# Storing a convolution tail and final states untransposed, and a key weight laid out by numpy, in a hybrid SSD and MLA decode step

## The chip, the cores and the metric

One core of a Trainium2 chip runs the whole program. The metric is device time in microseconds (us) of one execution. Work done by numpy on the host, before the inputs are handed over or after the outputs come back, is not in it. The kernel before was run three times: 1915.88, 1918.3 and 1923.65 us, median 1918.3.

## The reference, cut to what matters

Two layers follow each other, each as `h = h + Mixer(RMSNorm(h))`: a Mamba-2 SSD layer and an MLA attention layer. Both run on a prompt of 1024 positions and on 8 samples of 8 positions. Three pieces of the reference matter here:

```
xbc, new_buf = causal_conv(xbc, conv_buf, conv_w, conv_b)    # new_buf: last 3 rows before the convolution, 4096 channels
y, new_state = ssd_scan(xs, dt, a_head, bm, cm, ssm_state)   # new_state: (heads 32, headdim 64, state 128)
q_lat = einsum('bqhn,chn->bqhc', q_nope, w_uk)               # absorb: the samples' queries into the latent space
```

`new_buf` and `new_state` are outputs, for the prompt (3 rows, one state) and for the samples (8 times 3 rows, 8 states). `w_uk` has the shape (256 latent, 16 heads, 64).

## The kernel before, in words

TensorE (PE) multiplies float32 by splitting each operand into a high and a low part and adding three products; these are the matmuls of `mm3` (L89) and `mm_tok` (L101). Transposes are matmuls against the identity `k.ident` in plain float32.

**SSD layer.** The 2048 channels and 32 heads fall into 8 groups. `Group` projects one group: four blocks of 128 channels (B, C, two of x) through `proj_piece` (tile `pj`, L89), each put into a `raw` tile, convolved on DVE (L528), and its last 3 rows of the prompt and of each sample copied by POOL into `ct`, 128 channels x 4 blocks x 27 rows (L521, L522). After the fourth block `conv_out` transposes the four pieces of `ct` to rows (tile `ctp`, L536), copies them to `co` on DVE (L538), and stores `co` by six DMAs of the SP queue (L541, L542). Then `gates` projects z (tile `pz`, L101). While group g+1 is projected, `ssd_chunks` and `ssd_states` scan group g: eight chunks of 128 positions, then the samples. The running state `S` (128 state rows x 4 heads x 64) is, after the eighth chunk, transposed in two pieces (tile `pf`, L669), copied to `fo` by ACT (L671) and stored (L672). `ctp`, `pf` and the scan's own transposes share PSUM slots with the tag `tr`, two of them in this layer; `co` takes one of the two slots of the tag `raw`. During the last group `last_steps` loads pieces of the output weight (tile `wor`, L772) into slots of the same tag `raw`, and ACT and DVE split them (L773, L774).

**MLA layer.** `Heads.prep_q` prepares one head at a time: it transposes the samples' queries (tile `qs`, L1357), transposes the head's 256 x 64 key weight out of the tile `wkr` in two pieces into the same PSUM tile (L1359), copies the result to `wt` on ACT (L1366), transposes the prompt's queries (L1374) and last multiplies `wt` by the samples' queries (tile `ql...p`, L1380). `wt` has two buffers, so head h takes the buffer of head h-2. `wkr` is loaded once per four heads (L1282) into a single buffer, and is also split into high and low parts for the prompt's keys. `maxpass` takes row maxima, turns them with a transpose (tile `nmp`, L1417) and sends them through DRAM on the SP queue: a store `nd<-nr` (L1421) and a load `qTh<-nd` (L1422) that waits for it.

**What sets the order.** In the SSD layer and in the first part of MLA a scheduler orders every engine's instructions when the program is built. In the head loop (`mla_heads`) and after it PE and POOL keep the order in which the code is written; ACT, DVE and the SP queue are still ordered by the scheduler. Nearly all DMAs are issued by SP, in order: an issue that waits for a semaphore holds up all that stand behind it.

Of the kernel before, what the change touches and what calls it, by code (L numbers as in the profile page):

```python
# [8 lines left out]
F32 = mybir.dt.float32  # L9
# [13 lines left out]
DIN = 2048  # L23
# [7 lines left out]
RAW = 3 + SEQ + NB * (NT + 3)  # L31
# [51 lines left out]
PB = dict(PB1)  # L83
# [44 lines left out]
def split(k, hi, lo, src, eng=None, parts=0):  # L128
    nc = k.nc
    k.cast = nc.scalar.copy(hi, src)  # L130
    n = parts and hi.shape[1] // parts
    for a in range(parts):
        s = slice(a * n, a * n + n)
        (eng or nc.vector).tensor_tensor(lo[:, s], src[:, s], hi[:, s].bitcast(F32), op=ALU.subtract)
    if not parts:
        return (eng or nc.vector).tensor_tensor(lo, src, hi.bitcast(F32), op=ALU.subtract)  # L136
# [324 lines left out]
class Group:  # L461
# [69 lines left out]

    def conv_out(self):
        k, g, nc, gp = self.k, self.g, self.k.nc, self.gp
        p = self.psum.tile([128, 512], F32, tag="tr", name=f"ctp{g}", bufs=PB["tr"])
        for bi in range(4):
            nc.tensor.transpose(p[:27, bi * 128 : bi * 128 + 128], self.ct[:, bi], k.ident)  # L536
        co = self.rp.tile([128, RAW], F32, tag="raw", name=f"co{g}", bufs=2)[:27, :512]
        nc.vector.tensor_copy(co, p[:27])  # L538
        sc = k.O["s_conv"].rearrange("o b w c -> (o b w) c")
        for o, n, c in ((0, 128, DIN + 128 * g), (128, 128, DIN + 1024 + 128 * g), (256, 256, 256 * g)):  # L540
            nc.sync.dma_start(k.O["p_conv"][0, 0, :, c : c + n], co[0:3, o : o + n])  # L541
            nc.sync.dma_start(sc[:, c : c + n], co[3:27, o : o + n])  # L542

    def steps(self):
        yield from self.pair(0, self.g == 0)
# [37 lines left out]
def ssd_chunks(k, gr, pools):  # L583
    nc, I = k.nc, k.I
    sp, psum = pools
    g = gr.g
    S = None
    hs = slice(4 * g, 4 * g + 4)
    for i in range(9):
# [5 lines left out]
        tag = f"{g}_{i}"  # L595
        p = psum.tile([128, 512], F32, tag="tr", name="trp" + tag, bufs=PB["tr"])
# [45 lines left out]
        if not smp:  # L642
# [12 lines left out]
            S = S2  # L655
# [8 lines left out]
        nc.scalar.activation(xD[:m], y[:m], AF.Square, accum_out=k.yssq[:m, i, g : g + 1])  # L664
        nc.sync.dma_start(k.y_d[sl, 256 * g : 256 * g + 256], y[:m])
        if i == 7:
            pf = psum.tile([128, 512], F32, tag="tr", name="pf" + tag, bufs=PB["tr"])
            for pr in range(2):
                nc.tensor.transpose(pf[:, pr * 128 : pr * 128 + 128], S[:, pr * 128 : pr * 128 + 128], k.ident)  # L669
            fo = sp.tile([128, 256], F32, tag="fo", name="fo" + tag, bufs=1).rearrange("p (a n) -> p a n", a=2)  # L670
            nc.scalar.copy(fo, pf[:, :256].rearrange("p (a n) -> p a n", a=2))  # L671
            nc.sync.dma_start(k.O["p_ssm"][0, 0, 4 * g : 4 * g + 4].rearrange("(a h) p n -> (h p) a n", h=2), fo)  # L672
        yield


# [64 lines left out]
def ssd_scan(k, gr, pools):  # L740
    chunks, states = ssd_chunks(k, gr, pools), ssd_states(k, gr, pools)
    for c in SCAN:
        next(chunks if c == "c" else states)
        yield 21 / len(SCAN)
    drain(chunks)
    drain(states)
# [437 lines left out]
class Heads:  # L1184
# [161 lines left out]
    def prep_q(self, h):  # L1346
        k, nc, sp = self.k, self.k.nc, self.sp
        hg, pr, j = h // 4, h // 2, h % 2
        if j == 0 and pr < 2:
            self.load_q(pr)  # L1350
        if j == 1 and 0 < pr < 7:
            self.load_q(pr + 1)
        qt = self.qts[pr]
        if h == 2:
            nc.gpsimd.memset(self.qT[2][1][96:98].bitcast(F32), 0.0)
        p = self.wt(f"qs{h}")
        nc.tensor.transpose(p[:96, :64], qt[:64, 8, 96 * j : 96 * j + 96], k.ident[:64, :64])  # L1357
        for c in range(2):
            nc.tensor.transpose(p[:64, 128 + c * 128 : 256 + c * 128],  # L1359
                                self.wkr[:, c, 64 * (h % 4) : 64 * (h % 4) + 64], k.ident)  # L1360
        qsn = sp.tile([64, 64], F32, tag="qsn", name=f"qsn{h}", bufs=2)
        nc.vector.tensor_copy(qsn, p[:64, :64])
        qv = k.qpr[:, :, NT * h : NT * h + NT]
        split(k, qv[0:32], qv[64:96], p[64:96, :64].rearrange("p (b t) -> p b t", t=NT))
        wt = sp.tile([64, 256], F32, tag="wt", name=f"wt{h}", bufs=2)
        nc.scalar.copy(wt, p[:64, 128:384])  # L1366
        yield
        if 1 < h < 4:
            self.ones_rows(h)
        qh, ql = self.q_of(h)  # L1370
        for c in range(2):
            p = self.wt(f"qT{h}{c}")
            for i in range(4):
                nc.tensor.transpose(p[:96, i * 128 : i * 128 + 128], qt[:, 4 * c + i, 96 * j : 96 * j + 96], k.ident)  # L1374
            cs = slice(512 * c, 512 * c + 512)
            split(k, qh[:96, cs], ql[:96, cs], p[:96])
            yield
        pl = self.wt(f"ql{h}p")
        for c in range(2):
            nc.tensor.matmul(pl[:, c * 64 : c * 64 + 64], wt[:, c * 128 : c * 128 + 128], qsn,  # L1380
                             start=True, stop=True)
        src = pl[:, :128].rearrange("p (c b t) -> p c b t", c=2, t=NT)
        split(k, *(x[:, :, :, NT * h : NT * h + NT] for x in (k.qlh, k.qll)), src)
        yield
# [684 lines left out]
def consts():  # L2069
# [21 lines left out]
_INS = ["x_prompt", "x_sample", "state_ssm", "state_conv", "cache_ckv", "cache_kpe", "page_table", "norm_w",  # L2091
        "final_norm_w", "ssd_w_in", "ssd_conv_w", "ssd_conv_b", "ssd_dt_bias", "ssd_a_log", "ssd_d", "ssd_norm_w",
        "ssd_w_out", "mla_w_in", "mla_q_norm_w", "mla_kv_norm_w", "mla_w_uq", "mla_w_uk", "mla_w_uv", "mla_w_out"]
_OUTS = [("y_prompt", (1, 1024, 1024)), ("y_sample", (8, 8, 1024)), ("p_ssm", (1, 1, 32, 64, 128)),
         ("p_conv", (1, 1, 3, 4096)), ("p_ckv", (1, 1, 1024, 256)), ("p_kpe", (1, 1, 1024, 32)),
         ("s_ssm", (1, 8, 32, 64, 128)), ("s_conv", (1, 8, 3, 4096)), ("s_ckv", (1, 8, 8, 256)),
         ("s_kpe", (1, 8, 8, 32))]


# [26 lines left out]
```

## Time and profile before

| | |
|---|---|
| three runs | 1915.88, 1918.3, 1923.65 us; median 1918.3 |
| profiled execution | span 1915.0 us from its first to its last instruction; the page prints no time around the span |
| PE busy | 1887.4 us, 99% of the span, 12023 matmuls |
| PE weight loads (PEld) busy | 1728.1 us, 90% |
| DVE, ACT, POOL busy | 1208.5, 1101.1, 823.3 us (63%, 57%, 43%) |
| granted TensorE clock, mean | 0.997 |

A matmul's record runs from its start to a modelled end, and the next matmul may start long before that end. So the busy time says that PE is nearly always holding some matmul, and what one matmul costs in a full stream is read from the distance of starts, not from the record's length. A line of the page such as L89 can be a helper's line, used by many tiles.

### The profile page before, as it was taken

What the parts mean: (1) busy time and instruction counts of PE and PEld (TensorE: products, weight loads), DVE (VectorE), ACT (ScalarE), POOL (GpSimd) and SP (SyncE); (2) the same over time, 40 slices, a digit from 0 to 9 for tenths busy, and PEclk for the clock granted to TensorE, in tenths of its full rate; (3) what the DMA queues carried; (4) which work ended last, traced back from release to release, by engine and by line L of the source; (5) the groups of instructions that cost most, each with busy time, mean ns of one, the idle gap of its engine ahead of it and who ended that gap; (6) DMA issues with size and microseconds to landing.
All of it is one profiled execution on the core that took longest, in us unless ns stands there. A gap on an engine that the chain in (4) does not pass through costs nothing.

```text
span 1915.0 us, 33672 instructions
## 1 busy us (share of the span) xinstructions
PE 1887.4 (99%) x12023; PEld 1728.1 (90%) x12023; DVE 1208.5 (63%) x2500; ACT 1101.1 (57%) x2528; POOL 823.3 (43%) x1116
## 2 busy tenths in 40 slices
PE   8999999999999999999999999999999999999998
PEld 7999999999999999888788998898888887888887
DVE  5557676757676767765534214566887878666665
ACT  6467666767666666732214323436777777755552
POOL 2447555555655555453004322103443434764551
PEclk9999999999999999999999999999999999999999
DMA  5223323332323232644424662233111112664451
GB/s 165 54 79 91 94 83 94 88 106 83 101 84 99 85 99 78 212 158 175 166 110 133 209 226 75 69 110 95 47 52 41 53 41 58 228 204 142 146 170 37
DMA packets 183967, 212.51 MB, mean 111 GB/s; under 512 B 19148, under 2 KB 147928, under 8 KB 182776
## 3 DMA queue, kind: packets, MB, share of 16 engines
q1 hardware_dynamic: 177304, 185.32, 31.1%
q0 software_dynamic: 6416, 24.91, 3.8%
q8 instruction: 95, 1.56, 0.3%
q14 instruction: 72, 0.59, 0.1%
q10 hardware_dynamic: 80, 0.13, 0.0%
HBM read 151.76 MB, written 58.52 MB: 110 GB/s over the span
## 4 chain that ended last, share of the span: by engine, by line
PE 90%; DMA 3%; DVE 3%; ACT 3%; issue 1%; POOL 0%; SPq 0%; POOLq 0%; DVEq 0%; ACTq 0%
PE pj L89 24%; PE pz L101 8%; PE pq L101 6%; PE pob L101 5%; PE p L101 5%; PE poa L101 4%; PE py L640 3%; PE sc L89 3%; PE o L89 2%; PE sc L1402 2%; PE o L1465 2%; PE o L1467 2%; PE st L1434 2%; PE st L1435 2%; PE st L1436 2%; PE o L1466 2%
## 5 line engine op out<-in xcount | busy, mean ns | idle before, releaser
L89 PE MATMUL pj<-xl,wih 128*128 128x384 f32 (+1 forms) x768 | 255.4, 333 | 0.0
L89 PE MATMUL pj<-xh,wih 128*128 128x384 f32 (+1 forms) x768 | 252.9, 333 | 1.2 <-ACT xh L276 0.8
L89 PE MATMUL pj<-xh,wil 128*128 128x384 f32 (+1 forms) x768 | 252.9, 329 | 0.0
L1448 POOL TENSOR_TENSOR tl<-P,th 128x384 fp32r<-128x384 f32 (+1 forms) x96 | 90.6, 944 | 232.3 <-ACT P L1446 186.6
L528 DVE SCALAR_TENSOR_TENSOR acc<-raw,vec,acc 128x1112 f32<-128x1112 f32 x96 | 141.6, 1476 | 15.3 <-ACT acc L524 14.4
L89 PEld LDWEIGHTS pj<-xh,wih 128*128 128x128 f32 x768 | 143.8, 188 | 2.6 <-ACT xh L276 1.4
L89 PEld LDWEIGHTS pj<-xl,wih 128*128 128x128 f32 x768 | 144.5, 188 | 1.0
L89 PEld LDWEIGHTS pj<-xh,wil 128*128 128x128 f32 x768 | 144.5, 188 | 0.5
L101 PE MATMUL pz<-wih,xh 128*128 128x256 f32 x504 | 143.3, 288 | 1.4 <-ACT z L569 1.4
L101 PE MATMUL pz<-wil,xh 128*128 128x256 f32 (+1 forms) x504 | 139.8, 283 | 0.0
L1445 ACT ACTIVATE th<-st 128x512 fp32r<-128x512 f32 x192 | 94.6, 493 | 66.6 <-PE st L1441 50.9
L101 PE MATMUL pz<-wih,xl 128*128 128x256 f32 x448 | 128.5, 287 | 0.0
L1733 POOL TENSOR_TENSOR kvl<-pgr,kvh 128x256 fp32r<-128x256 f32 x128 | 97.8, 791 | 70.6 <-ACT kvh L1731 70.3
L635 ACT ACTIVATE M<-M,tok 128x128 f32<-128x128 f32 (+1 forms) x288 | 90.4, 386 | 51.4 <-DVE M L631 51.2
L136 DVE TENSOR_TENSOR wil<-wraw,wih 128x512 fp32r<-128x512 f32 x88 | 74.4, 851 | 38.2 <-ACT wih L130 31.7
L101 PEld LDWEIGHTS pz<-wih,xh 128*128 128x128 f32 x504 | 95.9, 190 | 2.3 <-ACT z L569 1.8
L1446 ACT ACTIVATE P<-st 128x512 f32<-128x512 f32 x192 | 93.5, 487 | 0.0
L101 PEld LDWEIGHTS pz<-wil,xh 128*128 128x128 f32 (+1 forms) x504 | 92.8, 184 | 0.1
L101 PE MATMUL p<-w,oh 128*128 128x512 f32 (+3 forms) x304 | 88.8, 386 | 0.6 <-DVE h L1983 0.6
L616 POOL TENSOR_TENSOR xdd<-xsT,tok 128x256 f32<-128x256 f32 x64 | 50.0, 781 | 86.4 <-ACT xsT L602 83.3
L101 PEld LDWEIGHTS pz<-wih,xl 128*128 128x128 f32 x448 | 85.4, 191 | 0.7
L1448 DVE TENSOR_TENSOR tl<-P,th 128x512 fp32r<-128x512 f32 x96 | 72.1, 752 | 18.9 <-ACT P L1446 18.7
(830 smaller groups left out, 6212.5 us busy)
## 6 DMA issues: line engine op xcount, KB each, us to landing
wraw<-in_ssd_w_in SPq DMA_DIRECT2D x92, 256.0 KB
M<-acs_d SPq DMA_DIRECT2D x64, 256.0 KB
s<-in_state_ssm SPq DMA_DIRECT2D x32, 256.0 KB
y_d<-y SPq DMA_DIRECT2D x64, 128.0 KB
out_s_ssm<-s SPq DMA_DIRECT2D x32, 256.0 KB
q_d<-qt SPq DMA_DIRECT2D x32, 192.0 KB
qp<-q_d SPq DMA_DIRECT2D x8, 768.0 KB
wraw<-in_ssd_w_out SPq DMA_DIRECT2D x10, 512.0 KB
```

The lines of the kernel that those rows point to most:

```text
L89: nc.tensor.matmul(out, a, b, start=(i == 0), stop=(i == n - 1))
L101: nc.tensor.matmul(o, a, b, start=(j == 0), stop=(j == len(ops) - 1))
L136: return (eng or nc.vector).tensor_tensor(lo, src, hi.bitcast(F32), op=ALU.subtract)
L528: last = nc.vector.scalar_tensor_tensor(acc, raw[:, j : j + n], k.convw[j][:, blk : blk + 1], acc, op0=ALU.mult, op1=ALU.add)
L616: nc.gpsimd.tensor_tensor(v3(xdd), v3(xsT), hb(2), op=ALU.mult)
L635: nc.scalar.activation(M[:m, h, :m], M[:m, h, :m], AF.Exp, bias=tk[:, 0, 4 * g + h : 4 * g + h + 1])
L640: nc.tensor.matmul(py[:m, h * 64 : h * 64 + 64], M[:m, h, :m], xsT[:m, h * 64 : h * 64 + 64], start=True, stop=True)
L1402: nc.tensor.matmul(ps[:, :n], qh[:96, 128 * i : 128 * i + 128], kh[:96, 512 * c : 512 * c + n], start=True, stop=True)
L1445: nc.scalar.activation(th[:, :n], ps[:, :n], AF.Exp, scale=SCALE)
L1446: nc.scalar.activation(P[:, :n], ps[:, :n], AF.Exp, scale=SCALE)
L1448: eng.tensor_tensor(tl[:, :n], P[:, :n], th[:, :n].bitcast(F32), op=ALU.subtract)
L1733: nc.gpsimd.tensor_tensor(rl[:, j], raw[:, j], rh[:, j].bitcast(F32), op=ALU.subtract)
```

## The change

Three transposes leave the chip. `conv_out` now only stores `ct` as it lies, with one DMA per group, into a new output `conv` of shape (8, 128, 4, 27); numpy takes `p_conv` and `s_conv` out of it. The final state `S` is stored as it lies into an output of shape (8, 128, 256), and numpy turns it. The key weight comes a second time as an input `c_wukt` of shape (16, 64, 256), turned by numpy, and each head's 64 KB is loaded into `wt` by a DMA. The PSUM tiles `ctp` and `pf`, the tile `co` and the copies L538, L671 and L1366 go.

```diff
     def conv_out(self):
         k, g, nc, gp = self.k, self.g, self.k.nc, self.gp
-        p = self.psum.tile([128, 512], F32, tag="tr", name=f"ctp{g}", bufs=PB["tr"])
-        for bi in range(4):
-            nc.tensor.transpose(p[:27, bi * 128 : bi * 128 + 128], self.ct[:, bi], k.ident)
-        co = self.rp.tile([128, RAW], F32, tag="raw", name=f"co{g}", bufs=2)[:27, :512]
-        nc.vector.tensor_copy(co, p[:27])
-        sc = k.O["s_conv"].rearrange("o b w c -> (o b w) c")
-        for o, n, c in ((0, 128, DIN + 128 * g), (128, 128, DIN + 1024 + 128 * g), (256, 256, 256 * g)):
-            nc.sync.dma_start(k.O["p_conv"][0, 0, :, c : c + n], co[0:3, o : o + n])
-            nc.sync.dma_start(sc[:, c : c + n], co[3:27, o : o + n])
+        nc.sync.dma_start(k.O["conv"][g], self.ct)
...
         if i == 7:
-            pf = psum.tile([128, 512], F32, tag="tr", name="pf" + tag, bufs=PB["tr"])
-            for pr in range(2):
-                nc.tensor.transpose(pf[:, pr * 128 : pr * 128 + 128], S[:, pr * 128 : pr * 128 + 128], k.ident)
-            fo = sp.tile([128, 256], F32, tag="fo", name="fo" + tag, bufs=1).rearrange("p (a n) -> p a n", a=2)
-            nc.scalar.copy(fo, pf[:, :256].rearrange("p (a n) -> p a n", a=2))
-            nc.sync.dma_start(k.O["p_ssm"][0, 0, 4 * g : 4 * g + 4].rearrange("(a h) p n -> (h p) a n", h=2), fo)
+            nc.sync.dma_start(k.O["p_ssm"][g], S)
...
         p = self.wt(f"qs{h}")
+        wt = sp.tile([64, 256], F32, tag="wt", name=f"wt{h}", bufs=2)
+        nc.sync.dma_start(wt, k.I["c_wukt"][h])
         nc.tensor.transpose(p[:96, :64], qt[:64, 8, 96 * j : 96 * j + 96], k.ident[:64, :64])
-        for c in range(2):
-            nc.tensor.transpose(p[:64, 128 + c * 128 : 256 + c * 128],
-                                self.wkr[:, c, 64 * (h % 4) : 64 * (h % 4) + 64], k.ident)
         qsn = sp.tile([64, 64], F32, tag="qsn", name=f"qsn{h}", bufs=2)
         nc.vector.tensor_copy(qsn, p[:64, :64])
         qv = k.qpr[:, :, NT * h : NT * h + NT]
         split(k, qv[0:32], qv[64:96], p[64:96, :64].rearrange("p (b t) -> p b t", t=NT))
-        wt = sp.tile([64, 256], F32, tag="wt", name=f"wt{h}", bufs=2)
-        nc.scalar.copy(wt, p[:64, 128:384])
```

How the instructions stand now is shown at three places. Line numbers of the changed kernel are up to 16 lower for the same code (L600 is L592, L733 is L720, L772 is L759, L1421 is L1405, L1422 is L1406). First PE in group 4, where the transposes of `ct` stood. `trp` is the scan's transpose of chunk 5, `pz` the z projection, `sn` the samples' state. Before:

```order
L600 MATMUL trp_5_5874<-ident,acc_3809 128x128
L536 MATMUL ctp_5941<-ident,ct_5076 27x128 x3
L101 MATMUL pz<-wih,xh 128x256
L101 MATMUL pz<-wil,xh 128x256
L733 MATMUL sn_801_5842<-bb_81_5817,x_81_5811 128x512
```

Now, at the same place:

```order
L592 MATMUL trp_5_5811<-ident,acc_3763 128x128
L101 MATMUL pz<-wih,xh 128x256
L101 MATMUL pz<-wil,xh 128x256
L101 MATMUL pz<-wih,xl 128x256
L101 MATMUL pz<-wih,xh 128x256
L101 MATMUL pz<-wil,xh 128x256
L720 MATMUL sn_801_5779<-bb_81_5754,x_81_5748 128x512
```

The three transposes are gone and `sn` stands three matmuls of z later. Counted from the first `py` of the group, the `py` of chunk 5 stood behind 446 matmuls and stands behind 456 now, and that of the samples stood behind 641 and stands behind 635.

Second the SP queue in the head loop, around the maxima of head 4. `og_d` is an output store, `nd4_0` and `nd4_1` are the two halves of the maxima, `wt7` is the key weight of head 7. Before:

```order
L1479 DMA og_d_12461<-og0_15555 64x512
L1421 DMA nd4_0_16685<-nr4_0_16683 8x128
L1422 DMA qTh1_14502<-nd4_0_16685 2x512
L1421 DMA nd4_1_16768<-nr4_1_16766 8x128
L1422 DMA qTh1_14502<-nd4_1_16768 2x512
```

Now:

```order
L1463 DMA og_d_12325<-og0_15415 64x512
L1405 DMA nd4_0_16537<-nr4_0_16535 8x128
L1406 DMA qTh1_14366<-nd4_0_16537 2x512
L1345 DMA wt7_16935<-in_c_wukt 64x256
L1405 DMA nd4_1_16620<-nr4_1_16618 8x128
L1406 DMA qTh1_14366<-nd4_1_16620 2x512
```

The load of `wt7` stands between the two halves of head 4, and in the same way, three heads ahead of their use, stand those of the heads 4 to 15. The load of `wkr` (L1282) moved too: that for heads 4 to 7 stood among the maxima of head 1 and now stands between the stores of the fourth and fifth `qt` of the query projection.

Third the SP queue in the last projected group, around the loads `wor`. `s06`, `s07` are sample states, `M6` the decay rows, `co7`/`ct7` the convolution tails. Before:

```order
L736 DMA out_s_ssm<-s06_810_9755 128x4x128
L541 DMA out_p_conv<-co7_9882 3x128
L542 DMA out_s_conv<-co7_9882 24x128
L541 DMA out_p_conv<-co7_9882 3x128
L542 DMA out_s_conv<-co7_9882 24x128
L541 DMA out_p_conv<-co7_9882 3x256
L542 DMA out_s_conv<-co7_9882 24x256
L714 DMA s07_800_10457<-in_state_ssm 128x4x128
L772 DMA wor0_9967<-in_ssd_w_out 128x1024
```

Now:

```order
L622 DMA M6_5_9724<-acs_d_1104 128x512
L759 DMA wor0_9841<-in_ssd_w_out 128x1024
L622 DMA M6_6_9873<-acs_d_1104 128x512
L657 DMA y_d_81<-y6_3_9458 128x256
L622 DMA M6_7_10041<-acs_d_1104 128x512
L657 DMA y_d_81<-y6_4_9544 128x256
L534 DMA out_conv<-ct7_8898 128x108
L723 DMA out_s_ssm<-s06_810_9641 128x4x128
```

`co7` no longer takes a slot of the tag `raw`, so `wor0` stands six DMAs ahead of the state's store instead of eight behind it.

## Rows read from the trace of the kernel before

**Rows 1.** The page's part 1: busy time, share of the span, instructions.

```profile
PE 1887.4 (99%) x12023; PEld 1728.1 (90%) x12023; DVE 1208.5 (63%) x2500; ACT 1101.1 (57%) x2528; POOL 823.3 (43%) x1116
```

**Rows 2.** The page's part 4: the chain that ended last, by engine.

```profile
PE 90%; DMA 3%; DVE 3%; ACT 3%; issue 1%; POOL 0%; SPq 0%; POOLq 0%; DVEq 0%; ACTq 0%
```

**Rows 3.** Windows: stretch, length, busy PE, PEld, DVE, ACT, POOL; clock, DMA, GB/s.

```profile
300.00:400.00 100.00, 99.64 (x740) 98.10 (x738) 68.59 (x109) 67.23 (x166) 52.73 (x83) 1.00 0.31 90
750.00:850.00 100.00, 96.80 (x657) 86.41 (x656) 70.73 (x131) 60.26 (x142) 49.70 (x68) 1.00 0.53 176
1350.00:1450.00 100.00, 99.93 (x602) 87.20 (x601) 80.34 (x202) 76.89 (x174) 39.55 (x39) 1.00 0.17 48
```

**Rows 4.** Timeline of PE, group 4: start, length, engine, line, operation, tiles, shape.

```profile
464.09 0.49 PE L536 MATMUL ctp<-ident,ct 128*27 128x128 f32 x3
464.33 0.36 PE L101 MATMUL pz<-wih,xh 128*128 128x256 f32 x1
464.54 0.28 PE L101 MATMUL pz<-wil,xh 128*128 128x256 f32 x1
464.65 0.48 PE L733 MATMUL sn<-bb,x 96*128 96x512 f32 x1
```

**Rows 5.** Timeline of PE in the head loop, at one head's key weight.

```profile
1405.84 0.41 PE L1359 MATMUL qs<-ident,w 128*64 128x128 f32 x2
1406.01 0.31 PE L1402 MATMUL sc<-kTh,qTh 96*128 96x128 f32 x1
1406.15 0.27 PE L1465 MATMUL o<-th,Vh 128*128 128x128 f32 x1
1406.26 0.28 PE L1466 MATMUL o<-th,Vl 128*128 128x128 f32 x1
```

**Rows 6.** Lines L536, L669, L1359: count, then ns min/median/max, first and last start.

```profile
L536 PE MATMUL ctp<-ident,ct x32: 270/272/292, 57.2 to 757.2; 128*27 128x128 f32 x32
L669 PE MATMUL pf<-ident,S x16: 270/271/272, 198.6 to 885.4; 128*128 128x128 f32 x16
L1359 PE MATMUL qs<-ident,w x32: 272/285/301, 1252.8 to 1593.5; 128*64 128x128 f32 x32
```

**Rows 7.** Lines L538, L671, L1366, in the same columns.

```profile
L538 DVE COPY co<-ctp x8: 669/669/672, 78.3 to 759.5; 27x512 f32<-27x512 f32 x8
L671 ACT COPY fo<-pf x8: 355/373/375, 199.0 to 885.7; 128x256 f32<-128x256 f32 x8
L1366 ACT COPY wt<-qs x16: 353/366/371, 1256.1 to 1597.5; 64x256 f32<-64x256 f32 x16
```

**Rows 8.** Line L542 on the SP queue, in the same columns.

```profile
L542 SPq DMA_DIRECT2D out_s_conv<-co x24: 302/302/332, 79.3 to 761.9; - x24
```

**Rows 9.** Waits of PE: who waited, for whom, us in total, times, longest.

```profile
PE ctp L536 <- POOL ct L522: 1.0, 1, 1.0
```

**Rows 10.** Timeline of the SP queue in the head loop, at the maxima of head 4.

```profile
1391.13 0.27 SPq L1421 DMA_DIRECT2D nd<-nr  x1
1392.34 0.23 SPq L1422 DMA_DIRECT2D qTh<-nd  x1
1397.17 0.26 SPq L1421 DMA_DIRECT2D nd<-nr  x1
```

**Rows 11.** Line L1380 for heads 5 and 7, columns as in rows 6.

```profile
L1380 PE MATMUL ql5p<-qsn,wt x4: 272/272/320, 1393.0 to 1393.4; 64*128 64x64 f32 x4
L1380 PE MATMUL ql7p<-qsn,wt x4: 272/272/320, 1433.5 to 1433.9; 64*128 64x64 f32 x4
```

**Rows 12.** Timeline of DVE in the query projection.

```profile
1230.72 0.69 DVE L136 TENSOR_TENSOR w<-w,w 128x512 fp32r<-128x512 f32 x1
1233.73 0.22 DVE L1179 TENSOR_TENSOR qt<-u,w 128x64 f32<-128x64 f32 x1
```

**Rows 13.** The chain that ended last, its longest DMA pieces between 770 and 800.

```profile
773.51 4.68 DMA wor<-in_ssd_w_out
790.18 6.14 DMA yta<-y_d
```

More of the change, by code (lines that the diff above doesn't have):

```diff
@@ L2093 @@
         "ssd_w_out", "mla_w_in", "mla_q_norm_w", "mla_kv_norm_w", "mla_w_uq", "mla_w_uk", "mla_w_uv", "mla_w_out"]
-_OUTS = [("y_prompt", (1, 1024, 1024)), ("y_sample", (8, 8, 1024)), ("p_ssm", (1, 1, 32, 64, 128)),
-         ("p_conv", (1, 1, 3, 4096)), ("p_ckv", (1, 1, 1024, 256)), ("p_kpe", (1, 1, 1024, 32)),
-         ("s_ssm", (1, 8, 32, 64, 128)), ("s_conv", (1, 8, 3, 4096)), ("s_ckv", (1, 8, 8, 256)),
+_OUTS = [("y_prompt", (1, 1024, 1024)), ("y_sample", (8, 8, 1024)), ("p_ssm", (8, 128, 256)),
+         ("conv", (8, 128, 4, 27)), ("p_ckv", (1, 1, 1024, 256)), ("p_kpe", (1, 1, 1024, 32)),
+         ("s_ssm", (1, 8, 32, 64, 128)), ("s_ckv", (1, 8, 8, 256)),
          ("s_kpe", (1, 8, 8, 32))]
@@ L2116 @@
     given.update(consts())
+    given["c_wukt"] = np.ascontiguousarray(given["mla_w_uk"][0].transpose(1, 2, 0))
     for n, a in given.items():
@@ L2124 @@
     r = run_bass_kernel_spmd(nc, [arrays], core_ids=[0])
-    return tuple(r.results[0]["out_" + n] for n, _ in _OUTS)
+    o = {n: r.results[0]["out_" + n] for n, _ in _OUTS}
+    rows = o["conv"].transpose(3, 2, 0, 1)
+    rows = np.concatenate([rows[:, 2:].transpose(0, 2, 1, 3).reshape(27, 2048), rows[:, 0].reshape(27, 1024),
+                           rows[:, 1].reshape(27, 1024)], 1)
+    o["p_conv"] = rows[:3].reshape(1, 1, 3, 4096)
+    o["s_conv"] = rows[3:].reshape(1, 8, 3, 4096)
+    o["p_ssm"] = o["p_ssm"].reshape(8, 128, 4, 64).transpose(0, 2, 3, 1).reshape(1, 1, 32, 64, 128)
+    return tuple(o[n] for n in ("y_prompt", "y_sample", "p_ssm", "p_conv", "p_ckv", "p_kpe", "s_ssm", "s_conv",
+                                "s_ckv", "s_kpe"))
```

## The prediction

> **What bounds the kernel now.** I read the share of busy time first: PE holds a matmul for 1887.4 of 1915.0 us, and no other engine passes 63% [rows 1]. Then the chain of work that ended last: 90% of it runs over PE [rows 2]. Then the stretches in which the change sits. In the middle of the SSD groups PE is busy 99.64 of 100 us, in the head loop 99.93, both at full granted clock, and only where the last group meets the output projection does it drop to 96.80 [rows 3]. So a PE instruction that goes should be seen in the span nearly in full, and an ACT, DVE or SP instruction that goes should be seen only where PE was waiting for it. A busy share this high hides short waits, since a record's modelled end reaches over the next start; therefore the price of a matmul is taken from starts.
>
> **What goes from PE.** 32 transposes of `ct`, 16 of `S`, 32 of the key weight: 80 [rows 6]. In group 4 three transposes start at 464.09, and the second z matmul behind them starts at 464.54, 0.45 us later. One z matmul takes 0.11 to 0.12 (464.54 to 464.65), which leaves 0.33, or 0.11 each [rows 4]. The 16 of `S` have the same 128 columns and the same record of 0.27 us [rows 6]; I give them the same 0.11. For the key weight, two start at 1405.84; two 128-column matmuls later it is 1406.26, with one of them costing 0.11 (1406.15 to 1406.26). So the first of them effectively begins at 1406.04, which leaves 0.20 for two, 0.10 each [rows 5]. Sum: 48 x 0.11 + 32 x 0.10 = 5.3 + 3.2 = 8.5 us. No matmul is added.
>
> Here the row and a rule differ. The record of each of these transposes lasts 0.27 us [rows 6], while the starts stand 0.11 apart [rows 4]. The Trainium skill ("TensorE: Matmul & The Clock Gate", Part 4: PE-mode transpose) says that a transpose takes about 275 ns within a kernel. The trace agrees with it as a length and not as a distance. By the length the sum would be 22 us, by the distance it is 8.5; the first is a rival below.
>
> **What goes from ACT and DVE.** Eight copies of 0.67 us on DVE, 5.4 us, and on ACT 8 of 0.37 and 16 of 0.37, 8.8 us [rows 7]. In the groups ACT and DVE are busy two thirds of the time, in the head loop 77% and 80% [rows 3]; the next matmuls of PE cover these copies. I cost them at nothing, with an upper bound where the cover fails: the 16 key weight copies delay PE in full, 16 x 0.37 = 5.9 us.
>
> **Waits that go.** PE waited once, 1.0 us, for POOL to fill `ct` [rows 9]; that is gone with its reader, and the z matmuls behind need nothing of POOL. I count 1.0. `ctp` and `pf` no longer hold one of the two `tr` slots, and `co` no `raw` slot. What this is worth no row shows. The place where it shows best is the last group: `wor0` is issued ahead of the states' stores, and DMA pieces for `wor` and for the y rows behind it sit in the chain for 4.68 and 6.14 us [rows 13], in a stretch where PE idles 3.2 of 100 us [rows 3]. The gain lies between nothing (what PE lacks there is y, not the weight) and 3.2; I take 1.0, nearer nothing, since most of the chain there is ACT and DVE work that stays.
>
> **What is added on the SP queue.** Of 48 stores of the convolution tail, at 0.30 us per issue as in [rows 8], 8 remain, and 8 stores of the state stay 8. SP gains some 12 us of issue time in the SSD layer; PE waits for none of it. 16 loads of 64 KB come into the MLA layer, each about 0.3 us of issue. Two questions decide whether they cost anything.
>
> Do they arrive in time? `wt7` stands behind the load of head 4's first maxima, which issued at 1392.34 [rows 10], and takes the buffer of `wt5`, which head 5's matmuls read from 1393.0 on, the last from 1393.4 [rows 11]. So it issues near 1394. I have no row for a 64 KB load. From below: the store of head 4's maxima at 1391.13 had landed when the load waiting for it issued at 1392.34, 1.2 us for 4 KB [rows 10]. From above: the 512 KB piece of 6.1 us [rows 13]. I take 3, between both and nearer the small one. Even at 6.1 it lands at 1400, and head 7 multiplies at 1433.5 [rows 11]: 33 us of cover.
>
> Do they hold up what stands behind them? While `wt7` waits for its buffer, SP can't issue the second half of head 4's maxima. That stood at 1397.17 [rows 10], some 3 us behind the release near 1394, and it can't be ready sooner: its transpose comes after head 5's matmuls in PE's written order. So: nothing. The early `wkr` load could hold the stores of `qt`, on whose buffers ACT waits. It needs the split of the first key weight on DVE, from 1230.72 for 0.69; the next `qt` is ready only at 1233.95 [rows 12]. Covered by 2.5 us.
>
> The `ct` and `S` tiles are now read by a DMA rather than by PE, so they come free a few us later. `ct` is next written about a block projection into the next group, and `S` has two buffers in turn, the next write of this one being the second chunk of the next group. Nothing.
>
> **Sum.** 8.5 + 1.0 + 1.0 = 10.5 us. The span of the profiled execution goes from 1915.0 to 1904.5. The page prints no time around the span; the three runs lie 0.9 to 8.7 us above it, and the median 1918.3 lies 3.3 above. I carry the difference over to the median: 1918.3 - 10.5 = 1907.8 us, 0.55% less. For this kernel 0.5% (9.6 us) is about what a measurement can tell from no change; the three runs of before are 0.4% apart.
>
> **Rivals.**
>
> *Given back in the schedule.* The scheduler fills the freed places with z matmuls from later on, so the scan's chain through ACT, DVE and POOL is no earlier, and the group ends when the scan does. For it: the SSD chain leaves PE in pieces of ACT, DVE and DMA, 10% of the whole [rows 2]. Against it: PE is 99.64% busy there [rows 3], and the samples' `py` now stands behind 635 instead of 641 matmuls, just the six that went. If the 48 SSD transposes give nothing and the rest does: 3.2 + 1.0 = 4.2, so 1914.1.
>
> *Slower: the scan reaches its end late.* In groups 2 to 5 the `py` of chunk 5 stands behind 456 matmuls instead of 446, though four transposes ahead of it are gone: 14 z matmuls more, 14 x 0.12 = 1.7 us later [rows 4]. If chunks 6, 7 and the samples then follow late and PE has run out of z, PE pays it. The break-even lies at 10.5 / 7 = 1.5 us per group over seven groups. Paid twice (chunks 5 and 6 both stand later), 3.4 x 7 = 23.8 less 10.5 gives +13.3: 1931.6. Against it: chunk 7 and the samples stand earlier than before, so there is z left to fill with.
>
> *The transposes cost their whole record.* 80 x 0.27 = 21.6, with the two waits 23.6: 1894.7. For it, only the length of the record; against it the starts in rows 4 and 5. If each starts something slow behind it, some of this could come back.
>
> *The change doesn't do what it says:* a late load takes the transpose's place, PE waiting at `ql`. With 14 heads at 3 us less 10.5 this would be +31. The 33 us of cover leave it under 1 in 100.
>
> **How the numbers follow.** Forecast (gain of 7 to 14 us, 1904 to 1911, which takes in that other waits shrink or appear by 3 us either way): 0.70. Given back: 0.17. Slower: 0.08. Whole record, or copies that PE did wait for in full (5.9 more): 0.05. The range that leaves out 2 in 10 reaches up through the given-back case to 1915, and down to 1918.3 - 10.5 - 5.9 - 2.2 (the rest of the 3.2) = 1900: 1900 to 1915. Faster by over 0.5% needs less than 1908.7: nearly two thirds of the forecast's 0.70, 0.46, and the last case's 0.05, together 0.51. Within 0.5%: the rest of the forecast 0.24, and the given-back case 0.17, together 0.41. Slower by over 0.5%: 0.08.
>
> **What would show it.** PE with 80 matmuls fewer, its busy share still 98% or more. From the transposes of chunk 5 on, PE's starts in group 4 run 0.33 us sooner per three transposes, and the SSD groups follow each other about 0.6 us more closely. The end of the SSD part comes about 5 to 7 us sooner, the head loop is 3 us shorter. `ql` waits for no DMA. Wrong would be: a group as long as before with new waits of PE at `py` or `st` (given back, or slower); a row in which `ql` waits for `wt`; a gain of more than 15 us, which would mean that the copies or the PSUM slots were being waited for behind the busy share.

## The result and the profile after

The changed kernel takes 1924.4 us, median of 6 runs (1920.3 to 1927.6); the kernel before, run beside it on the same chip, 1915.8 (1914.3 to 1923.7). The ratio is 1.0034, 95% interval 1.0018 to 1.0049: slower by 3.5 to 9.4 us where 10.5 less were forecast, and above the range of 1900 to 1915. The profiled execution has a span of 1922.4 us against 1915.0.

The page's part 1 and the first line of its part 4 for the changed kernel, which answer to [rows 1, 2]:

```profile
PE 1885.7 (98%) x11943; PEld 1721.2 (90%) x11943; DVE 1211.8 (63%) x2492; ACT 1092.1 (57%) x2504; POOL 829.6 (43%) x1116
...
PE 82%; DMA 5%; DVE 4%; ACT 4%; issue 2%; POOL 1%; SPq 0%; POOLq 0%; DVEq 0%; ACTq 0%
```

The 80 matmuls are gone (12023 to 11943). But the chain that ends last leaves PE more often: 82% instead of 90% runs over it. The windows of [rows 3] say where (stretch, length, busy PE, PEld, DVE, ACT, POOL, clock, DMA, GB/s):

```profile
300.00:400.00 100.00, 98.27 (x726) 96.65 (x725) 66.18 (x108) 65.04 (x162) 54.62 (x86) 1.00 0.30 88
750.00:850.00 100.00, 96.44 (x662) 86.95 (x661) 73.46 (x127) 61.22 (x147) 51.08 (x67) 1.00 0.50 165
1350.00:1450.00 100.00, 99.93 (x586) 86.36 (x585) 81.08 (x203) 74.53 (x170) 41.27 (x41) 1.00 0.18 51
```

The head loop is as full as it was. In the groups PE went from 99.64 to 98.27 us busy in 100. The waits of PE (who waited, for whom, us in total, times, longest) name the places:

```profile
PE cb L620 <- DVE yo L716: 4.1, 7, 1.0
PE pj L89 <- ACT raw L511: 3.0, 4, 0.9
PE pv L713 <- DVE sl L136: 2.3, 3, 1.3
...
PE st L89 <- POOL xddl L136: 1.9, 2, 1.2
```

In the kernel before, the first of these took 1.1 us, and for the copy at L511, which the second names, PE waited nowhere. The wait for `ct` [rows 9] is gone; these four grew or came.

For the length of the groups I use one row: ACT's Silu over `acc`, which ends each of a group's two pairs. Its first and last start between 240 and 748 us bound the same work in each kernel, five groups from the second pair of group 1 on. Before, then after (count, ns min/median/max, first and last start):

```profile
L484 ACT ACTIVATE acc<-acc x11: 2061/2066/2066, 243.4 to 731.3; 128x2224 f32<-128x2224 f32 x11
```

```profile
L484 ACT ACTIVATE acc<-acc x11: 2062/2064/2067, 245.6 to 739.2; 128x2224 f32<-128x2224 f32 x11
```

That is 487.9 and 493.6 us: five groups became 5.7 us longer, where 5 x 0.66 less were forecast. One trace has noise of its own here: three pairs of kernels with the same order of the SSD layer (before and the first experiment, the changed kernel and the fourth, the fifth and the eighth) take 487.9 and 489.3, 493.6 and 494.6, 487.2 and 488.9 us. So a difference of 1 or 2 us by this row alone says nothing. By the single starts that this row sums up, the halves in which the transposes of `ct` stood got shorter (the one from 341.2 in the kernel before from 33.2 to 32.3 us), the others longer (the one from 276.6 from 64.7 to 66.5). The long half ahead of these five groups isn't in the row; it grew as well, from 64.2 to 67.3 us.

**What makes the long halves longer.** The chain that ended last, in the changed kernel between 607 and 617 (start, length, what):

```profile
607.79 2.76 PE pj L89 x16
610.55 3.55 DMA M<-acs_d
...
614.12 0.70 DVE M L623
...
615.16 0.97 ACT M L627 x3
616.13 0.37 ACT raw L511
...
616.55 0.61 PE pj L89 x2
```

From 610.55 to 616.50 the chain runs over a load of decay rows `M`, DVE's add, ACT's exponentials, and then ACT's copy of a projection block from PSUM (`raw`). PE isn't waiting for the rows here. It waits for the copy, which frees a place for the next `pj`, and the copy stands behind the exponentials in ACT's queue. ACT's timeline, then PE's (in brackets the idle time before, and what ended it):

```profile
614.85 1.28 ACT L627 ACTIVATE M<-M,tok 128x128 f32<-128x128 f32 x4 [2.39 <-DVE M L623]
616.04 0.46 ACT L511 COPY raw<-pj 128x384 f32<-128x384 f32 x1
```

```profile
616.55 0.44 PE L89 MATMUL pj<-xh,wih 128*128 128x384 f32 x1 [0.83 <-ACT raw L511]
```

The load is late because of SP's order. SP's timeline in the changed kernel, then in a kernel with the order of before (the fifth experiment), at the same place:

```profile
606.97 3.47 SPq L321 DMA_DIRECT2D wraw<-in_ssd_w_in  x2
610.55 0.45 SPq L622 DMA_DIRECT2D M<-acs_d  x1
```

```profile
600.11 0.38 SPq L321 DMA_DIRECT2D wraw<-in_ssd_w_in  x1
600.61 0.43 SPq L622 DMA_DIRECT2D M<-acs_d  x1
603.61 0.37 SPq L321 DMA_DIRECT2D wraw<-in_ssd_w_in  x1
```

The second weight load has to wait some 3 us for its buffer. In the order of before `M` is issued ahead of it, in the changed kernel behind it. This swap stands at five borders of groups. The border ahead of them doesn't have it: in the long half that starts at 178.3 in the changed kernel, PE waits for POOL's `xddl` (1.2 us) and DVE's `sl` (2.1 us) instead.

### The profile page after: what moved, and what is told of

It reads as the page before. It is cut to its first block, busy times and chain, and to the rows that moved or that the text cites. A ratio compares the mean times of both kernels' runs of the same rounds, so it can differ in the third digit from the quotient of the medians.

```text
span 1922.4 us, 33435 instructions
## 1 busy us (share of the span) xinstructions
PE 1885.7 (98%) x11943; PEld 1721.2 (90%) x11943; DVE 1211.8 (63%) x2492; ACT 1092.1 (57%) x2504; POOL 829.6 (43%) x1116
## 4 chain that ended last, share of the span: by engine, by line
PE 82%; DMA 5%; DVE 4%; ACT 4%; issue 2%; POOL 1%; SPq 0%; POOLq 0%; DVEq 0%; ACTq 0%
PE pj L89 20%; PE pz L101 8%; PE pq L101 6%; PE pob L101 5%; PE p L101 5%; PE poa L101 3%; PE sc L89 2%; PE py L632 2%; PE o L89 2%; DMA M<-acs_d 2%; PE sc L1386 2%; PE o L1449 2%; PE st L1418 2%; PE o L1451 2%; PE st L1419 2%
## 5 line engine op out<-in xcount | busy, mean ns | idle before, releaser
L528 DVE SCALAR_TENSOR_TENSOR acc<-raw,vec,acc 128x1112 f32<-128x1112 f32 x96 | 145.5, 1517 | 11.8 <-ACT acc L524 10.5
L136 DVE TENSOR_TENSOR wil<-wraw,wih 128x512 fp32r<-128x512 f32 x88 | 68.8, 792 | 34.6 <-ACT wih L130 31.0
L1432 DVE TENSOR_TENSOR tl<-P,th 128x512 fp32r<-128x512 f32 x96 | 76.1, 793 | 19.5 <-ACT P L1430 19.1
```

Of the source, the lines that this page charges most:

```text
L528: last = nc.vector.scalar_tensor_tensor(acc, raw[:, j : j + n], k.convw[j][:, blk : blk + 1], acc, op0=ALU.mult, op1=ALU.add)
L1432: eng.tensor_tensor(tl[:, :n], P[:, :n], th[:, :n].bitcast(F32), op=ALU.subtract)
```

## The experiments

Each kernel was timed in five rounds against the kernel before on the same chip; its ratio to that, with the interval, is what is compared. One permille is 1.9 us.

**Parts of the change alone.** Four kernels, each with only the named hunks of the diff: the key weight, the tail, the state, and tail with state. The fence has the line that each adds, and in parentheses what goes. I had two theories: that the state's store brought the loss ("state"), or the tail's missing transposes ("tail").

```diff
 e1: + nc.sync.dma_start(wt, k.I["c_wukt"][h])        (transposes and copy of wkr go)
 e2: + nc.sync.dma_start(k.O["conv"][g], self.ct)     (ctp, co and six stores go)
 e3: + nc.sync.dma_start(k.O["p_ssm"][g], S)          (pf and fo go)
 e4: e2 and e3 together
```

Key weight. 

> Only the key weight comes turned; convolution tail and final state stay as in the kernel before. Both theories put the loss of the changed kernel (+7 to +9 us) into the SSD groups and none into the head loop. Theory 'state' and theory 'tail' alike: 2 to 4 us shorter than before (32 transposes of 0.10), SSD groups of the same length as before, head loop 2 to 3 us shorter. If instead the loads or the head loop carried part of the loss, this kernel would be equal to before or slower.

Measured 0.9996 (0.9986 to 1.0007): it does no harm that the times can tell, but the 3.2 us aren't there either.

Tail. 

> Only the convolution tail is stored as it lies. Theory 'state' (the loss comes with the store of the final state: its copy on ACT is gone, and at the border of two groups SP's queue now has both weight loads ahead of the decay rows of chunk 3, so ACT holds the copy of a projection block behind exponentials that wait, and PE waits about 1.1 us per group at pj): no loss here, 2 to 5 us shorter than before (32 transposes of 0.11 and the wait of 1.0). Theory 'tail' (the four transposes that are gone let z matmuls move forward, chunk 5's py stands behind 456 instead of 446 matmuls, and the scan ends late): 5 to 9 us longer than before.

Measured 1.0042 (1.0029 to 1.0056): slower, as only "tail" expected.

State. 

> Only the final state is stored as it lies. Theory 'state': 7 to 11 us longer than before, the stretches between a group's pair and the next group's first pair longer by 1 to 3 us each, with waits of PE at pj for ACT's raw copy of 3 us in total or more. Theory 'tail': 1 to 2 us shorter than before (16 transposes of 0.11), no new wait at pj.

Measured 1.0036 (1.0023 to 1.0050): slower, as only "state" expected, with 2.1 us of waits at `pj` for the copy where it expected 3 or more.

Both. 

> Tail and state stored as they lie, the key weight transposed on PE as before. Both theories: the changed kernel without its gain in the head loop, so 9 to 12 us longer than before, and 2 to 4 us longer than the changed kernel. Rival: if the key weight loads did harm that reaches back, it would equal the changed kernel or be shorter.

Measured 1.0029 (1.0020 to 1.0038). That is less than the 9 to 12 us that both theories expected. Both fall as the one cause: either part alone costs 7 to 8 us, and the two together no more than one. The SSD layer has the same order here as in the changed kernel, and the time is the same within the intervals, as the rival of a harm by the key weight loads expected; but alone those loads did no harm, so what is missing is their gain. The two parts have in common that the scheduler made a new order of the layer. The new orders aren't the same: with the tail alone PE waits at `sn`, `cb` and `pv` and not at `pj` for the copy at L511, with the state alone at `pj`, at `cb`, and once for 2.7 us at `s0p`. So the next experiments took the order itself.

**The order of before.** The changed kernel, with an order edge from each instruction of the SSD layer to the next one on its engine, for the order that the kernel before has (code shortened):

```diff
         layer_mla(k)
+        pin(tc, ORDERS)   # ORDERS: per engine, the places of the instructions in the order of before
...
+        for a, b in zip(seq, seq[1:]):
+            tc.add_manual_dep(traced[b], traced[a].name, DependencyInfo(NoSync, DATA), reason="pin")
```

> The changed kernel with the instructions of the SSD layer pinned, on every engine and on SP's queue, to the order that they have in the kernel before, less those that are gone. Theory 'order' (what the change removes is worth what was forecast, and the new order of the instructions, which follows from it, costs 16 to 19 us): 7 to 11 us shorter than before. Rival 'free transposes' (they lay in stretches in which PE would have waited anyway, and the loss comes from the new stores or from the freed slots): within 3 us of before or longer, whatever the order.

Measured 0.9986 (0.9974 to 0.9999), median 1914.9. The same work in another order is 9 us faster than the changed kernel (1.0034 less 0.9986), and the waits at `pj`, `pv` and `st` are gone or small. The edges themselves add no work: both kernels have 11943 matmuls, 2492 instructions on DVE and 2504 on ACT. Yet only 2.7 us (0.2 to 5.0) are gained on before, a quarter of what was forecast: neither theory is right alone.

**The same without the key weight.** 

> Tail and state stored as they lie, in the order of the kernel before on every engine, the key weight transposed on PE as before. Theory 'order': 48 transposes of 0.11 and the wait of 1.0, so 5 to 7 us shorter than before, and 2 to 3.5 us longer than the kernel with the order of before and the turned key weight. Rival 'free transposes': within 2 us of before.

Measured 0.9985 (0.9974 to 0.9995): as much as with the turned key weight. So the SSD part gives 2.9 us (1.0 to 5.0) of its 5 to 7, between the theory and its rival, and the key weight nothing that these runs can tell.

**Orders mixed.** First PE from before and all else from after, then the reverse, with PE left to the scheduler.

> The changed kernel with PE alone in the order of the kernel before; ACT, DVE, POOL and SP keep the order of the changed kernel, pinned. If the loss lies in the queues of the other engines (raw copies behind exponentials that wait for decay rows, yo late on DVE): 1920 to 1926 us, as long as the changed kernel, with the same waits of PE at pj and cb. If it lies in PE's own order (py of chunk 5 ten matmuls later): 1906 to 1912 us.

Measured 1.0298 (1.0279 to 1.0316), far outside both: PE waits at `st` for ACT's `xddh` 9.9 us and for others. PE's order of before doesn't fit the queues of after; this run decides nothing between the two.

> The reverse: ACT, DVE, POOL and SP in the order of the kernel before, PE as the scheduler then puts it. If the loss lies in the queues of the other engines: 1906 to 1912 us, without the waits at pj and cb. If it lies in PE's order: 1918 to 1926 us.

Measured 0.9980 (0.9966 to 0.9993), median 1912.7: as good as the full order of before, and without the waits at `pj`. So the loss goes with the queues of the other engines; it doesn't settle the place of chunk 5, since the scheduler then put its `py` behind 432 matmuls.

**The decay rows alone.** On SP's queue, at five borders, two neighbours swapped; all else pinned. The fence sketches one border. In the first kernel the order of before gets the swap, in the second the order of after loses it:

```diff
 order of before, SP:                 order of after, SP:
   y_d <- y (samples)                   y_d <- y (samples)
   wraw                                 wraw
-  M (chunk 3)                        + M (chunk 3)
   wraw                                 wraw
+  M (chunk 3)                        - M (chunk 3)
```

> The kernel with the order of before, with one thing of the changed order put in: on SP's queue, at five borders of groups, the load of the decay rows of chunk 3 stands behind the next weight load instead of ahead of it (five swaps of two neighbours). Theory 'decay rows' (that swap makes ACT's exponentials late, ACT holds the raw copy behind them, PE waits at pj): the stretches after the odd pairs longer by 0.8 to 1.5 us each with waits of PE at pj, in all 4 to 8 us longer than with the order of before, so 1919 to 1923 us. Rival 'many small ones' (the loss is spread over the queues, none of the swaps is worth a lot): within 2 us of the order of before, 1913 to 1917 us.

> The reverse: the changed kernel with its own order everywhere, pinned, but the decay rows of chunk 3 ahead of the weight load again at the five borders. Theory 'decay rows': 4 to 8 us shorter than the changed kernel, 1916 to 1920 us, waits of PE at pj for ACT's raw copy gone. Rival 'many small ones': 1922 to 1926 us.

Measured 1.0017 (1.0007 to 1.0028), 5.9 us more than the order of before, and 1.0015 (1.0005 to 1.0024), 3.6 us less than the changed kernel, just under the 4 to 8 expected and with these intervals only just clear of nothing. By the row of the Silu, the first and then the second, against 487.2 us for the order of before (242.7 to 729.9) and 493.6 for the changed kernel:

```profile
L484 ACT ACTIVATE acc<-acc x11: 2061/2063/2066, 242.3 to 738.1; 128x2224 f32<-128x2224 f32 x11
```

```profile
L484 ACT ACTIVATE acc<-acc x11: 2061/2065/2067, 244.6 to 733.6; 128x2224 f32<-128x2224 f32 x11
```

495.8 us with the swap put in, 489.0 with it taken out: +8.6 and -4.6 in these executions. PE's waits in the first, then in the second kernel:

```profile
PE pj L89 <- ACT raw L511: 5.4, 5, 1.8
```

```profile
PE cb L620 <- DVE yo L716: 4.2, 7, 1.0
PE pv L713 <- DVE sl L136: 2.8, 3, 1.3
```

Five swaps, five waits at `pj` for the copy at L511, in an order that had none; and in the order of after none without them. The theory holds from both sides. What stays in the second kernel against the order of before (2.9 permille, 5.6 us) goes with waits for DVE's `yo` and `sl`, 2.6 and 2.0 us more than there. That these are its cause is read from the trace alone; no kernel had only DVE's order exchanged.

**All of SP's queue.** 

> PE, ACT, DVE and POOL in the order of before, the whole SP queue of the SSD layer in the order of the changed kernel. If SP's queue alone carries the loss: 1922 to 1926 us. If it is ACT's, DVE's and POOL's order as much: 1914 to 1919 us.

Measured 1.0064 (1.0050 to 1.0077). With SP's order of after in it, the order of before is slower than the changed kernel, and slower than either expectation. The five groups are as long as with the five swaps alone (242.2 to 737.4, 495.2 us); the rest comes behind them, up to the head loop, where the last group meets the output projection: 528.1 us against 521.3, with waits of PE at `poa` and `pob` for DVE's `xra` of 3.5 us (0.8 in the order of before). Why `xra` is late there wasn't tried. So the parts don't add up to the whole: SP's order alone costs 15 us among the other queues of before, all five orders together 9.

**The covered wait.** In the order of before, without the transposes of `ct`, the half groups in which they stood are no shorter in these five groups. The reason is `sn`, which waits for POOL's `bb`. POOL and PE, group 4, in the order of before without the transposes:

```profile
462.27 1.54 POOL L695 TENSOR_TENSOR bb<-b,blk 96x512 fp32r<-96x512 f32 x1 [3.12 <-DVE b L693]
```

```profile
463.86 0.50 PE L720 MATMUL sn<-bb,x 96*128 96x512 f32 x1 [0.37 <-POOL bb L695]
```

`bb` ends at 463.81 and `sn` starts at once, after 0.37 us of idle PE. In the kernel before, the three transposes and two matmuls of z filled PE up to `sn` at 464.65 [rows 4]; their room has become the wait. The test: `sn` comes three z matmuls later, in six groups (a sketch of PE's order in one).

```diff
 PE:  trp, z, z,
-     sn,
      z, z, z,
+     sn,
```

> The order of before with one thing changed on PE: in six groups the samples' state matmul sn, which stands where the three transposes of the tail stood, comes three z matmuls later. Theory 'covered wait' (the three transposes lay over PE's wait for POOL's bb; gone, they leave that wait of 0.3 to 0.5 us): sn waits for POOL no longer, those half groups 0.3 us shorter each, 1.5 to 2.5 us in all, so 1911 to 1914 us. Rival: the half groups stay at 33.1 us, since something behind sn sets their end.

Measured 0.9974 (0.9960 to 0.9988), median 1912.2: 2.3 us less than the order of before, as expected, though the two intervals overlap. The trace is clearer: four of the five half groups went from 33.1 to 33.3 us to 32.7 or 32.8, the first stayed at 33.1, and in group 4 `sn` starts without a wait:

```profile
462.66 0.28 PE L101 MATMUL pz<-wil,xh 128*128 128x256 f32 x1
462.78 0.40 PE L720 MATMUL sn<-bb,x 96*128 96x512 f32 x1
```

This version beats both kernels, by 2.3 to 7.7 us before and by some 11.5 us after.

## Why the prediction was wrong

**The step that failed** is the one behind "what goes from ACT and DVE" and "what is added on the SP queue": that instructions off PE cost nothing and that SP's order changes nothing PE waits for ("PE waits for none of it"). The cost of the new order was put at nothing. I examined the SP queue of the head loop and of the last group, and PE's order in group 4, not the SP queue at the border of two groups. The new order costs 9 us (changed kernel against the order of before), 4 to 6 of them by the one swap at five borders. The second miss is the sum itself: in the order of before the change gains 2.7 us, not 10.5. The Trainium skill ("PSUM — Partial Sum Buffer", Engine vs sequencer instructions) says that the queues of ScalarE, VectorE and GpSimdE are strict FIFO (first in, first out). The trace agrees: the copy that PE needed ran at 616.13, right behind exponentials that it had no business with.

**The price of a transpose was borne out in one place, its worth was not.** In group 4 three transposes of 0.11 us went and a wait of 0.37 us came. Term by term, in the order of before:
- `ct`, forecast 32 x 0.11 = 3.5 us and 1.0 for its wait. The wait did go: the half in which it stood (from 143.2 us) takes 35.2 us instead of 36.0, and the short half of the first group 17.6 instead of 18.0. But the long halves that follow the two became 0.5 and 0.4 longer, so that the row's first Silu starts only 0.7 us sooner (242.7 for 243.4). In the five groups nothing was gained, since PE had to wait for `bb` at that place anyway. With `sn` moved behind z the five groups take 485.6 us (242.1 to 727.7) instead of 487.2, 1.6 less, where four transposes of 0.11 in each would be 2.2. The rival "given back in the schedule" said that they would bring nothing, but for another reason.
- `S`, forecast 2 x 0.11 in each long half: of the six from 179.2 us on, four are 0.2 us shorter, one is 0.1 and one 0.4 longer. That is 0.3 in all, where 1.3 were forecast, and less than two executions of one order differ by: not shown.
- Key weight, forecast 3.2. From the first transpose of a query to the last `ql`, without and with the turned weight (the two kernels in the order of before; lines L1344/L1346 `qs`, L1367/L1364 `ql15`):

```profile
L1344 PE MATMUL qs<-ident,qp x16: 229/257/260, 1257.4 to 1597.5; 64*96 64x64 f32 x16
L1367 PE MATMUL ql15p<-qsn,wt x4: 272/272/320, 1611.7 to 1612.1; 64*128 64x64 f32 x4
L1452 PE MATMUL o<-th,Vh x192: 220/392/507, 1317.0 to 1658.3; 128*128 128x512 f32 x96, 128*128 128x384 f32 x32, 128*128 128x256 f32 x32, 128*128 128x128 f32 x32
```

```profile
L1346 PE MATMUL qs<-ident,qp x16: 229/258/262, 1251.1 to 1589.9; 64*96 64x64 f32 x16
L1364 PE MATMUL ql15p<-qsn,wt x4: 272/272/320, 1604.0 to 1604.4; 64*128 64x64 f32 x4
L1449 PE MATMUL o<-th,Vh x192: 220/392/507, 1310.8 to 1651.7; 128*128 128x512 f32 x96, 128*128 128x384 f32 x32, 128*128 128x256 f32 x32, 128*128 128x128 f32 x32
```

354.7 and 353.3 us: 1.4 gained here, 2.2 in the changed kernel (352.9 against 355.1 before). Over all traces it is 354.6 to 355.1 us in the five that transpose on PE and 352.8 to 354.0 in the nine that don't. From there to the last `o` of this row it takes 46.2 us in all five, and 46.2 to 47.9 in the nine: up to 1.7 is given back in the last heads. In the changed kernel 1.1 of it is one wait for the load of maxima that PE has in none of the five; why that load is late isn't shown:

```profile
PE st L1418 <- DMA kTh<-nd: 1.1, 1, 1.1
```

Just behind that stretch, in the samples' attention, PE waits again in the order of before; the kernel that transposes on PE waits 0.06 us in all at the same two matmuls:

```profile
1655.54 0.39 PE L89 MATMUL o<-kvh,pTh 128*128 128x256 f32 x1 [0.42 <-ACT pTh L130]
1656.38 0.39 PE L89 MATMUL o<-kvh,pTl 128*128 128x256 f32 x1 [0.33 <-DVE pTl L136]
```

- Slots that come free, forecast 1.0: nothing to see. In the order of before `wor0` stands where it stood; in the changed kernel, where it stands earlier, the stretch from the last Silu of the row to the head loop takes 522.3 us against 521.4 before.

**What was right.** The loads of the key weight arrive in time and hold nothing up. The load of `wt7` was issued 1.4 us behind the load that belongs to the first half of head 4's maxima, and the second half followed 3.5 us later (SP's timeline of the changed kernel):

```profile
1399.93 0.23 SPq L1406 DMA_DIRECT2D qTh<-nd  x1
1401.28 0.48 SPq L1345 DMA_DIRECT2D wt<-in_c_wukt  x1
1404.75 0.26 SPq L1405 DMA_DIRECT2D nd<-nr  x1
```

No run shows a gain from the copies that went, as forecast, and the transposes' record of 0.27 us was not their price: no term came near 22 us, so the rival by the length that the Trainium skill gives ("TensorE: Matmul & The Clock Gate", Part 4: PE-mode transpose) is out.

**The rival "slower"** had the right sign and the wrong place. Chunk 5's `py` stands behind 456 matmuls in the kernel without the swap, too, and there PE never waits at chunk 5's `py`; its two waits at `py`, 0.4 and 0.3 us, are at other chunks of one group. The price was elsewhere; the part of it that was tried alone lies at a place in PSUM that ACT frees late.

Open is the rest of the order's cost, 3 to 6 of the 9 us: DVE's `yo` and `sl`, read from waits and not tried alone.

## What to carry to other kernels

When a scheduler makes the order, a small deletion can change it through a whole layer: compare each engine's queue, DMA queues first, at every border where two stages meet, and look for a load that now stands behind one that waits for a buffer; one order constraint there (here the load of the next weights behind the decay rows) may be worth more than the edit. Of a deleted instruction ask when the operands of the next one on its engine are ready: if they were only just ready, its time turns into a wait. And where an engine frees another's buffers, its in-order queue can be on the critical path even when it is 57% busy.

## What the runs showed of the hardware

TensorE's granted clock fell by half for some us at one place in seven of the 14 traces and not in the others. Behind a stretch in which PE had little to do, in the samples' attention after the head loop, the order of before shows 0.50 (1.2 GHz of 2.4), and the same without the turned key weight 1.00 (windows, columns as above):

```profile
1668.00:1671.00 3.00, 0.83 (x5) 0.53 (x4) 3.00 (x6) 0.00 (x0) 1.52 (x2) 0.93 1.03 331
1671.00:1674.00 3.00, 3.00 (x14) 2.91 (x14) 1.12 (x4) 2.27 (x5) 0.00 (x0) 0.50 1.01 408
```

```profile
1674.00:1677.00 3.00, 1.15 (x6) 0.89 (x7) 3.00 (x6) 0.00 (x0) 1.16 (x2) 1.00 1.03 263
1677.00:1680.00 3.00, 3.00 (x24) 2.50 (x24) 1.85 (x7) 2.64 (x5) 0.00 (x0) 1.00 1.01 403
```

In 3 us at the same place PE starts 14 matmuls at the one clock and 24 at the other. From the last `o` of the heads to the end it takes 259.3 to 262.0 us in the seven traces with the drop and 257.9 to 259.1 in the others: a difference as large as the terms of this sum, though other waits of that stretch differ too.
